# Attention's 1/sum moved to the output of a head pair, and rows normalised before their split

## The chip, the cores and the metric

The kernel runs on one core of a Trainium2 chip. The time is that of one execution in device microseconds. Five engines work side by side, each through its own queue in order: TensorE (PE: matmuls and transposes), VectorE (DVE), ScalarE (ACT), GpSimd (POOL) and SyncE (SP, which issues nearly all the DMAs here). They wait for each other by semaphores.

## The reference, cut to what matters

One encoder layer over two sequences of 512 tokens (`x_prompt` and `x_sample`, numbered 0 and 1 here) with 1024 channels: a SwiGLU feed-forward layer (FFN1), token mixing, a second feed-forward layer (FFN2), a final RMSNorm. All in fp32. What the change touches:

```python
def rms_norm(x, g):
    y = xf * lax.rsqrt(jnp.mean(xf * xf, axis=-1, keepdims=True) + EPS)
    return y * g
...
h = rms_norm(x, mix_norm)                  # x: (512, 1024) after FFN1
proj = h @ w_in                            # q, k, v, mLSTM's q, k, v, gates, o, g_att, g_mlstm
...
s = jnp.einsum('bqkgd,bskd->bkgqs', qi, k) * scale       # 8 heads of 64, 2 key/value heads
p = jax.nn.softmax(s, axis=-1)
o = jnp.einsum('bkgqs,bskd->bqkgd', p, v)
...
mem = mlstm_bidirectional(mq, mk, mv, gate_pre, mlstm_gate_bias, o_pre, mlstm_head_norm)
merged = sigmoid(g_att) * (att @ w_up_att) + sigmoid(g_mlstm) * (mem @ w_up_mlstm)
x = x + merged @ w_out
```

Both 1/rms (one number per token) and softmax's 1/sum (one per query and head) are factors that may stand before or after a matrix product.

## The kernel before

Activations lie with channels on the partitions: a tile of 128 channels by 512 tokens is a *row* here, 8 rows make a sequence. Every fp32 operand of a matmul is split into a high part in TensorE's rounded fp32 format (a copy on ACT) and the rest (a subtraction on DVE), and a product is three matmuls: high x high, high x low, low x high. `split` does this.

**FFN1's end.** `ffn_down` runs 28 steps of seven products each; `flush_` adds a bank of PSUM to the rows `xs[s]`. In the last steps the rows of sequence 0 are finished first, then those of sequence 1; `done1` is called for each finished row. It stores the row (`xbuf`, SP's queue) and adds its square to `accs[s]` (ACT squares, POOL adds, `sq_add`). For sequence 0 it also calls `emit_hl`: high part = row x gain `gm` on ACT (L144), low part by one scalar_tensor_tensor on DVE (L145), into `xh` and `xl`. So the rows are split without 1/rms. When the last row of sequence 0 is done, `mid_stats` makes 1/rms: transposes of `accs` and a sum (`col_sums`, L203 and L205), `rsqrt_cols` (Newton steps on 128x4, L171 to L192), and `bcast_cols`, which spreads it over a 128x512 row `R[s]` by four transposes (L213) and a copy (L219). `r[s]` has it by token on the partitions.

**Mixing.** `mix(s, ...)` is a generator; the two sequences are interleaved by hand (`next(m0)`, `next(m1)`), sequence 1's first projections with the end of sequence 0. The input projection runs in units: `tok_proj` puts tokens on the partitions (k/v and gates, q, mLSTM's v; lines 739 ff.), `win_cols` puts channels there (mLSTM's q and k, output gate, the two merge gates; L755). Its outputs lack 1/rms, and each eviction multiplies: with the column `r[s]` as ACT's scale in the first case, in the second by a tensor_tensor with `R[s]` on DVE (L918, L927, L1045, L1091) ahead of a split or a tanh. The weights of a unit are loaded on SP's queue, split (L239 on ACT, L240 on DVE) and parked in DRAM for sequence 1 (`load_w`).

**Attention.** `scores(h)`: for each of four blocks of 128 queries two matmuls into a PS bank, DVE's maximum (L1004), ACT's exponential with its sum (L1006), DVE's reciprocal (L1007) and DVE's scaling of the 128x512 exponentials (L1008). `attend(h)` turns them with TensorE transposes into a PT bank (L1020; there are two PT banks, also used by every other transpose), splits them, and multiplies with V into the bank `po` (L1028). The two halves of `po` are added into half of `af`, one row for a pair of heads (L1036, L1037); after the odd head `af` is split into `att`. Scores are one head ahead of `attend`. `fill` puts projection units from a queue (`att_gate`, `out_gate`) between heads.

**Order.** A list scheduler fixes each engine's order at build time, by priority; `shifted(n)` moves a part n places back. `T2(F32, "f2")` draws from a ring of four rows, `small` from rings of small tiles. In the merge of sequence 0 (`merge_mem`) `prep1` loads the rows of sequence 1 and splits them by `emit_hl`.

Of the kernel before, what the change touches and what calls it, by code (L numbers as in the profile page):

```python
# [16 lines left out]
P = 128  # L17
# [9 lines left out]
def encoder(ctx, tc, I, outs):  # L27
# [637 lines left out]
    def small(w, tag):  # L665
        return spool.tile([P, w], F32, tag=tag, bufs=2 if tag != "asm" else 6, name=nm(tag))
# [91 lines left out]
    OUT = 3  # L758

    def mix(s, xh, xl, early=None, extra=None, after=None):  # L760
# [8 lines left out]
        def F2(dtype=F32):  # L769
            return T2(dtype, "f2")  # L770

# [41 lines left out]
        def kv_done(pk):  # L813
            for b in range(4):
                nc.scalar.activation(kraw3[:, b, :], pk[b][:, 0:P], AF.Copy, scale=r[s][:, b:b + 1])
                nc.scalar.activation(Gt[:, b * 16:(b + 1) * 16], pk[b][:, 2 * P:2 * P + 16], AF.Copy,
                                     scale=r[s][:, b:b + 1])
                pv = pk[b][:, P:2 * P].rearrange("p (k e) -> p k e", k=HK)
                nc.scalar.activation(Vst[:, b, :, 0:DA], pv, AF.Copy, scale=r[s][:, b:b + 1])
                V_.scalar_tensor_tensor(Vst[:, b, :, DA:2 * DA], pv, r[s][:, b:b + 1], f(Vst[:, b, :, 0:DA]),  # L820
                                        op0=ALU.mult, op1=ALU.subtract)
# [11 lines left out]
        def q_done(pq):  # L833
            ssq = small(32, "ssq")
            for b in range(4):
                t = T2()
                nc.scalar.activation(t, pq[b], AF.Copy, scale=r[s][:, b:b + 1])
                sumsq(t, ssq[:, b * 8:(b + 1) * 8])
                qraw.append(t)
            rq.append(rstd_cols(ssq, 32, DA))  # L840
# [56 lines left out]
        def mem_values():  # L897
            def done(pvv):
                vm = A([P, 2, 4, S], F32R, "Vm")
                for b in range(4):  # L900
                    nc.scalar.activation(vm[:, 0, b, :], pvv[b], AF.Copy, scale=r[s][:, b:b + 1])
                    V_.scalar_tensor_tensor(vm[:, 1, b, :], pvv[b], r[s][:, b:b + 1], f(vm[:, 0, b, :]),
                                            op0=ALU.mult, op1=ALU.subtract)
                Vm.append(vm)
# [4 lines left out]
        def mem_qk(h, j):  # L909
            def done(pp):  # L910
# [6 lines left out]
                t = F2()  # L917
                V_.tensor_tensor(t, pp, R[s], op=ALU.mult)  # L918
                split(t, *qks[h][2 * j:2 * j + 2])
# [4 lines left out]
        def out_gate(h):  # L924
            def done(pp):
                og = T2(F32, "ac")
                V_.tensor_tensor(og, pp, R[s], op=ALU.mult)  # L927
                nc.scalar.activation(og, og, AF.Tanh, scale=0.5)
# [65 lines left out]

        def scores(h):
            hk = h // 4
            Ps = []
            for b in range(4):
# [4 lines left out]
                c = small(3, "asm")  # L1003
                V_.tensor_reduce(c[:, 0:1], p, axis=AX.X, op=ALU.max, negate=True)  # L1004
                e = T2()
                nc.scalar.activation(e, p, AF.Exp, bias=c[:, 0:1], accum_out=c[:, 1:2])  # L1006
                V_.reciprocal(c[:, 2:3], c[:, 1:2])  # L1007
                V_.tensor_scalar(e, e, c[:, 2:3], None, op0=ALU.mult)  # L1008
# [3 lines left out]
        def attend(h, Ps):  # L1012
# [25 lines left out]
            if h % 2:  # L1038
                split(af, att[:, h // 2, 0, :], att[:, h // 2, 1, :])
# [3 lines left out]
        def att_gate(d):  # L1043
            def done(pp):
                V_.tensor_tensor(mg[:, d, :], pp, R[s], op=ALU.mult)  # L1045
                nc.scalar.activation(mg[:, d, :], mg[:, d, :], AF.Tanh, scale=0.5)
# [41 lines left out]
        def mem_gate(d):  # L1088
            def done(pp):
                t = ths[d] = T2()  # L1090
                V_.tensor_tensor(t, pp, R[s], op=ALU.mult)  # L1091
                nc.scalar.activation(t, t, AF.Tanh, scale=0.5)
# [223 lines left out]
    def done1(s, d, _):  # L1316
        if s == 0:
            if d == 0:
                nhl[0] = xhl_tiles()
            emit_hl(xs[0][:, d, :], gm, d, *nhl[0])  # L1320
        nc.sync.dma_start(xbuf[s][:, d, :], xs[s][:, d, :])
        accs[s] = sq_add(xs[s][:, d, :], accs[s], "R")
        if s == 0 and d == KD - 1:
            mid_stats(0, 100, 140)
# [10 lines left out]
    def prep1(d):  # L1335
# [4 lines left out]
        emit_hl(xt, gm, d, *nhl[1])  # L1340
# [181 lines left out]
```

## Time and profile before

| what | value |
|---|---|
| median of 3 runs | 2084.76 us (2084.72 to 2087.68) |
| profiled execution, whole | 2083.45 us |
| its span in the profile | 2081.4 us |
| instructions | 27314 |
| PE busy | 2060.3 us (99%) |
| DVE busy | 1573.6 us (76%) |
| ACT busy | 895.4 us (43%) |
| POOL busy | 111.2 us (5%) |
| granted TensorE clock, mean | 0.999 |

The profile is of one execution; its times count from the start of the span. FFN1 takes the first 657 us, mixing the stretch from there to about 1431 us, FFN2 the rest. In a timeline row stand the start, the time until the end of the last of the merged instructions, engine, line and operation, the shape of output and input and the count; in brackets idle time before it and what ended it. PE's own ends are modelled, so for PE the distance from one start to the next is what a matmul costs. In a group row, after the count: busy us and mean ns of one, then the idle time of the engine ahead of it.

### The profile page before, as it was taken

To read this page: it belongs to the slowest core of one execution; us is meant where nothing else is said; L and a number is where in the kernel's file an instruction comes from. 1 tells how busy PE (TensorE), PEld (TensorE's weight loads), DVE (VectorE), ACT (ScalarE), POOL (GpSimd) and SP (SyncE) were. 2 spreads that over 40 slices of the span, in tenths; PEclk is the share of its full clock that TensorE was granted. 3 is DMA by queue.
4 is the path that set the end of the run, shared out by engine and by line. 5 is a ranking of instruction groups with operands and counts; after the bars stand their busy time and mean duration, and the time that the engine had idled before them with its cause. 6 is when DMAs were issued, how large, how long until landed. Compare 5 with 4: busy or idle time off the path is not lost.

```text
span 2081.4 us, 27314 instructions
## 1 busy us (share of the span) xinstructions
PE 2060.3 (99%) x9488; PEld 1694.0 (81%) x9488; DVE 1573.6 (76%) x2870; ACT 895.4 (43%) x1645; POOL 111.2 (5%) x122
## 2 busy tenths in 40 slices
PE   8999999999999999999999999999999999999998
PEld 6888888888888877888887788888888888888887
DVE  7888888786797899575568846555788888785797
ACT  6544444443234566463344543324444444442222
POOL 1000000001003012100120000002000000000010
PEclk9999999999999999999999999999999999999999
DMA  8656555699766655777685345677656555599753
GB/s 277 208 171 195 193 171 182 201 346 359 260 223 243 216 167 198 257 240 272 214 283 193 112 153 188 208 258 244 200 177 201 193 172 182 187 339 350 273 189 117
DMA packets 303161, 458.52 MB, mean 220 GB/s; under 512 B 20304, under 2 KB 170848, under 8 KB 302000
## 3 DMA queue, kind: packets, MB, share of 16 engines
q1 hardware_dynamic: 301152, 451.32, 64.4%
q0 software_dynamic: 1872, 5.46, 0.8%
q8 instruction: 75, 1.23, 0.2%
q14 instruction: 62, 0.51, 0.1%
HBM read 289.82 MB, written 166.89 MB: 219 GB/s over the span
## 4 chain that ended last, share of the span: by engine, by line
PE 92%; DVE 3%; DMA 3%; ACT 1%; issue 1%; SPq 0%; POOL 0%; DVEq 0%; ACTq 0%; POOLq 0%
PE mm L755 19%; PE pss L333 17%; PE pst L333 11%; PE mm L333 10%; PE mm L589 9%; PE pst L589 4%; PE pss L589 4%; PE mm L739 4%; PE pso L589 3%; PE pso L739 1%; PE pso L1028 1%; PE pso L1167 1%; PE pst L755 1%; PE pss L755 1%; PE pss L1117 1%; PE pst L1020 1%
## 5 line engine op out<-in xcount | busy, mean ns | idle before, releaser
L755 PE MATMUL mm<-xh,w 128*128 128x512 f32 x896 | 290.6, 394 | 0.0
L333 PE MATMUL pss<-xc,w 128*128 128x512 f32 x1056 | 256.4, 392 | 0.2 <-DVE t L364 0.2
L333 PE MATMUL mm<-xc,w 128*128 128x512 f32 x1056 | 253.5, 391 | 2.2 <-ACT w L291 1.4
L333 PE MATMUL pst<-xc,w 128*128 128x512 f32 x1056 | 253.8, 390 | 0.1
L333 PEld LDWEIGHTS pss<-xc,w 128*128 128x128 f32 x1056 | 197.0, 188 | 47.4 <-DVE t L364 6.7
L333 PEld LDWEIGHTS mm<-xc,w 128*128 128x128 f32 x1056 | 197.4, 188 | 45.2 <-ACT w L291 2.3
L333 PEld LDWEIGHTS pst<-xc,w 128*128 128x128 f32 x1056 | 198.2, 188 | 41.6 <-ACT t L368 0.5
L755 PEld LDWEIGHTS mm<-xh,w 128*128 128x128 f32 x896 | 167.4, 188 | 33.6
L589 PE MATMUL mm<-rt,w 128*128 128x512 f32 (+1 forms) x819 | 188.4, 385 | 0.0
L755 PE MATMUL mm<-xl,w 128*128 128x512 f32 x448 | 176.0, 393 | 0.0
L589 PEld LDWEIGHTS mm<-rt,w 128*128 128x128 f32 x819 | 151.4, 188 | 29.8
L291 ACT ACTIVATE w<-t 128x512 fp32r<-128x512 f32 x176 | 106.9, 627 | 138.6 <-issue 55.2
L292 DVE TENSOR_TENSOR w<-t,w 128x512 fp32r<-128x512 f32 x176 | 118.3, 689 | 55.1 <-ACT w L291 53.1
L333 PE MATMUL pss<-xc,f 128*128 128x512 f32 x528 | 126.9, 389 | 0.0
L333 PEld LDWEIGHTS pss<-xc,f 128*128 128x128 f32 x528 | 99.1, 188 | 20.6
L657 ACT ACTIVATE w<-wr 128x512 fp32r<-128x512 f32 x72 | 45.1, 632 | 138.6 <-PE pso L589 70.8
L657 ACT ACTIVATE w<-t 128x512 fp32r<-128x512 f32 x82 | 51.8, 632 | 107.6 <-PE pst L589 62.4
L755 PEld LDWEIGHTS mm<-xl,w 128*128 128x128 f32 x448 | 84.3, 188 | 16.7
L589 PE MATMUL pst<-rt,w 128*128 128x512 f32 x396 | 93.7, 389 | 0.0
L589 PE MATMUL pss<-rt,w 128*128 128x512 f32 x396 | 93.7, 389 | 0.0
L589 PEld LDWEIGHTS pst<-rt,w 128*128 128x128 f32 x396 | 74.3, 188 | 15.4
L589 PEld LDWEIGHTS pss<-rt,w 128*128 128x128 f32 x396 | 74.3, 188 | 15.4
(337 smaller groups left out, 3666.9 us busy)
## 6 DMA issues: line engine op xcount, KB each, us to landing
rt<-rbuf SPq DMA_DIRECT2D x154, 512.0 KB, 5.5
wpark<-w SPq DMA_DIRECT2D x104, 512.0 KB, 3.6
w<-wpark SPq DMA_DIRECT2D x104, 512.0 KB, 4.8
wr<-in_ffn_w_gate_dram SPq DMA_DIRECT2D x62, 512.0 KB, 5.3
rbuf<-tab SPq DMA_DIRECT2D x102, 256.0 KB, 3.8
wr<-in_ffn_w_up_dram SPq DMA_DIRECT2D x44, 512.0 KB, 4.7
rbuf<-f SPq DMA_DIRECT2D x72, 256.0 KB, 3.7
wr<-in_w_in_dram SPq DMA_DIRECT2D x36, 512.0 KB, 5.7
```

The source lines that it names most:

```text
L291: pin(nc.scalar.activation(t[:, 0], src, AF.Copy))
L292: pin(V_.tensor_tensor(t[:, 1], src, f(t[:, 0]), op=ALU.subtract))
L333: nc.tensor.matmul(p, a[:, k, :], xt[:, b, k, :], start=(first and k == 0 and i == 0), stop=(k == HK_ - 1 and i == 2), skip_group_check=True)
L589: nc.tensor.matmul(p, u[:, a, d * P:(d + 1) * P], r[:, b, ts], start=(first and q == 0 and k == 0), stop=(q == len(us) - 1 and k == 2), sk ...
L657: nc.scalar.activation(hi, src, AF.Copy)
L739: nc.tensor.matmul(p[b][:, :N], a[:, k, bs], w_[:, kl, :], start=(k == 0 and i == 0), stop=(k == KD - 1 and i == 2))
L755: nc.tensor.matmul(p, a[:, k, :], b, start=(k == 0 and i == 0), stop=(k == n - 1 and i == 2))
L1020: nc.tensor.transpose(p[:, b * P:(b + 1) * P], Ps[b][:, kb * P:(kb + 1) * P], ident)
L1028: nc.tensor.matmul(po, Vst[:, kv_, hk, :], w, start=(kv_ == 0 and i == 0), stop=(kv_ == 3 and i == 1))
L1117: nc.tensor.matmul(p, qk[a][:, isl], qk[b], start=(n == 0), stop=(n == 2))
L1167: nc.tensor.matmul(po, vm[:, a, t, hs_], b, start=(t == 0 and n == 0), stop=(t == 3 and n == 2))
```

## The change

- Softmax: the exponentials stay unscaled. The sums of a pair of heads go to one tile `asums` (128 x 4 blocks x 2 heads). After the odd head DVE takes one reciprocal of 128x8, ACT spreads it to a row `wide` (each value 64 times), TensorE turns that by four transposes into a PT bank, and DVE multiplies `af` with it before the split.
- `NORMED = (0, 1)`: both sequences' rows are multiplied with gain and 1/rms (`normed`, one scalar_tensor_tensor on DVE), and then split. For sequence 0 this is done for all eight rows after `mid_stats`, in place in `xs[0]`; `mid_stats` loses its shifts. For sequence 1 it is done in `prep1`.
- Evictions of the input projection lose the factor: `split_cols` is a plain split, tanh reads PSUM, mLSTM's q and k are split from PSUM.
- The ring of "asm" tiles has four buffers, was six.

```diff
@@ -663,7 +663,7 @@
     NEG = -1e30
 
     def small(w, tag):
-        return spool.tile([P, w], F32, tag=tag, bufs=2 if tag != "asm" else 6, name=nm(tag))
+        return spool.tile([P, w], F32, tag=tag, bufs=2 if tag != "asm" else 4, name=nm(tag))
 
     gm, g2 = [cpool.tile([P, KD], F32, name=nm("gain")) for _ in range(2)]
     gbias = cpool.tile([P, 16], F32, name="gbias")
@@ -756,6 +756,7 @@
         return p
 
     OUT = 3
+    NORMED = (0, 1)
 
     def mix(s, xh, xl, early=None, extra=None, after=None):
 
@@ -768,6 +769,22 @@
 
         def F2(dtype=F32):
             return T2(dtype, "f2")
+
+        def col_scale(b):
+            return 1.0 if s in NORMED else r[s][:, b:b + 1]
+
+        def split_cols(src, b, hi, lo):
+            if s in NORMED:
+                return split(src, hi, lo)
+            nc.scalar.activation(hi, src, AF.Copy, scale=r[s][:, b:b + 1])
+            V_.scalar_tensor_tensor(lo, src, r[s][:, b:b + 1], f(hi), op0=ALU.mult, op1=ALU.subtract)
+
+        def scaled_row(pp, to):
+            if s in NORMED:
+                return pp
+            t = to()
+            V_.tensor_tensor(t, pp, R[s], op=ALU.mult)
+            return t
 
         def win_cols(c0, done):
             return proj(win_v[:, :, c0:c0 + P], ("in", c0), xsrc, KD, done)
@@ -812,13 +829,11 @@
 
         def kv_done(pk):
             for b in range(4):
-                nc.scalar.activation(kraw3[:, b, :], pk[b][:, 0:P], AF.Copy, scale=r[s][:, b:b + 1])
-                nc.scalar.activation(Gt[:, b * 16:(b + 1) * 16], pk[b][:, 2 * P:2 * P + 16], AF.Copy,
-                                     scale=r[s][:, b:b + 1])
+                rsc = col_scale(b)
+                nc.scalar.activation(kraw3[:, b, :], pk[b][:, 0:P], AF.Copy, scale=rsc)
+                nc.scalar.activation(Gt[:, b * 16:(b + 1) * 16], pk[b][:, 2 * P:2 * P + 16], AF.Copy, scale=rsc)
                 pv = pk[b][:, P:2 * P].rearrange("p (k e) -> p k e", k=HK)
-                nc.scalar.activation(Vst[:, b, :, 0:DA], pv, AF.Copy, scale=r[s][:, b:b + 1])
-                V_.scalar_tensor_tensor(Vst[:, b, :, DA:2 * DA], pv, r[s][:, b:b + 1], f(Vst[:, b, :, 0:DA]),
-                                        op0=ALU.mult, op1=ALU.subtract)
+                split_cols(pv, b, Vst[:, b, :, 0:DA], Vst[:, b, :, DA:2 * DA])
             ssk = small(8, "ssk")
             sumsq(kraw, ssk)
             ko = rope_apply(kraw, rstd_cols(ssk, 8, DA), tabs[1], None)
@@ -834,7 +849,7 @@
             ssq = small(32, "ssq")
             for b in range(4):
                 t = T2()
-                nc.scalar.activation(t, pq[b], AF.Copy, scale=r[s][:, b:b + 1])
+                nc.scalar.activation(t, pq[b], AF.Copy, scale=col_scale(b))
                 sumsq(t, ssq[:, b * 8:(b + 1) * 8])
                 qraw.append(t)
             rq.append(rstd_cols(ssq, 32, DA))
@@ -898,9 +913,7 @@
             def done(pvv):
                 vm = A([P, 2, 4, S], F32R, "Vm")
                 for b in range(4):
-                    nc.scalar.activation(vm[:, 0, b, :], pvv[b], AF.Copy, scale=r[s][:, b:b + 1])
-                    V_.scalar_tensor_tensor(vm[:, 1, b, :], pvv[b], r[s][:, b:b + 1], f(vm[:, 0, b, :]),
-                                            op0=ALU.mult, op1=ALU.subtract)
+                    split_cols(pvv[b], b, vm[:, 0, b, :], vm[:, 1, b, :])
                 Vm.append(vm)
             return tok_proj(xh, xl, [(1792, 512)], 2, done)
 
@@ -914,9 +927,7 @@
                 elif s:
                     t = wpool.tile([P, 2, S], F32R, tag="wr", bufs=4, name=nm("qk"))
                     qks.setdefault(h, []).extend(t[:, i] for i in range(2))
-                t = F2()
-                V_.tensor_tensor(t, pp, R[s], op=ALU.mult)
-                split(t, *qks[h][2 * j:2 * j + 2])
+                split(scaled_row(pp, F2), *qks[h][2 * j:2 * j + 2])
             return win_cols((768, 1280)[j] + h * P, done)
 
         ogs = {}
@@ -924,8 +935,7 @@
         def out_gate(h):
             def done(pp):
                 og = T2(F32, "ac")
-                V_.tensor_tensor(og, pp, R[s], op=ALU.mult)
-                nc.scalar.activation(og, og, AF.Tanh, scale=0.5)
+                nc.scalar.activation(og, scaled_row(pp, lambda: og), AF.Tanh, scale=0.5)
                 G_.tensor_scalar(og, og, 1.0, hn[:, h:h + 1], op0=ALU.add, op1=ALU.mult)
                 ogs[h] = og
             return win_cols(2320 + h * P, done)
@@ -992,20 +1002,22 @@
         att = A([P, 4, 2, S], F32R, "att")
         afs = {}
 
+        asums = {}
+
         def scores(h):
             hk = h // 4
             Ps = []
+            if h % 2 == 0:
+                asums[h // 2] = small(8, "asum").rearrange("p (b u) -> p b u", u=2)
             for b in range(4):
                 p = PS()
                 for j in range(2):
                     nc.tensor.matmul(p, qT[:, h, b * P:(b + 1) * P], kv[:, hk * 2 + j, :],
                                      start=(j == 0), stop=(j == 1))
-                c = small(3, "asm")
-                V_.tensor_reduce(c[:, 0:1], p, axis=AX.X, op=ALU.max, negate=True)
+                c = small(1, "asm")
+                V_.tensor_reduce(c, p, axis=AX.X, op=ALU.max, negate=True)
                 e = T2()
-                nc.scalar.activation(e, p, AF.Exp, bias=c[:, 0:1], accum_out=c[:, 1:2])
-                V_.reciprocal(c[:, 2:3], c[:, 1:2])
-                V_.tensor_scalar(e, e, c[:, 2:3], None, op0=ALU.mult)
+                nc.scalar.activation(e, p, AF.Exp, bias=c, accum_out=asums[h // 2][:, b, h % 2:h % 2 + 1])
                 Ps.append(e)
             return Ps
 
@@ -1036,14 +1048,23 @@
             nc.scalar.activation(t[o0:o0 + DA, :], po[o1:o1 + DA, :], AF.Copy)
             V_.tensor_tensor(af[o0:o0 + DA, :], po[o0:o0 + DA, :], t[o0:o0 + DA, :], op=ALU.add)
             if h % 2:
-                split(af, att[:, h // 2, 0, :], att[:, h // 2, 1, :])
+                inv = asums[h // 2]
+                V_.reciprocal(inv, inv)
+                with shifted(30):
+                    wide = T2(F32, "f2")
+                    nc.scalar.activation(wide.rearrange("p (b u e) -> p b u e", u=2, e=DA),
+                                         inv.unsqueeze(3).to_broadcast([P, 4, 2, DA]), AF.Copy)
+                    pr = PT()
+                    for b in range(4):
+                        nc.tensor.transpose(pr[:, b * P:(b + 1) * P], wide[:, b * P:(b + 1) * P], ident)
+                    V_.tensor_tensor(af, af, pr, op=ALU.mult)
+                    split(af, att[:, h // 2, 0, :], att[:, h // 2, 1, :])
 
         mg = A([P, KD, S], F32, "mg")
 
         def att_gate(d):
             def done(pp):
-                V_.tensor_tensor(mg[:, d, :], pp, R[s], op=ALU.mult)
-                nc.scalar.activation(mg[:, d, :], mg[:, d, :], AF.Tanh, scale=0.5)
+                nc.scalar.activation(mg[:, d, :], scaled_row(pp, lambda: mg[:, d, :]), AF.Tanh, scale=0.5)
             return win_cols(2832 + d * P, done)
 
         queue.extend(att_gate(d) for d in range(KD))
@@ -1088,8 +1109,7 @@
         def mem_gate(d):
             def done(pp):
                 t = ths[d] = T2()
-                V_.tensor_tensor(t, pp, R[s], op=ALU.mult)
-                nc.scalar.activation(t, t, AF.Tanh, scale=0.5)
+                nc.scalar.activation(t, scaled_row(pp, lambda: t), AF.Tanh, scale=0.5)
             return win_cols(3856 + d * P, done)
 
         def merge_mem(d):
@@ -1314,14 +1334,14 @@
     box()
 
     def done1(s, d, _):
-        if s == 0:
-            if d == 0:
-                nhl[0] = xhl_tiles()
-            emit_hl(xs[0][:, d, :], gm, d, *nhl[0])
         nc.sync.dma_start(xbuf[s][:, d, :], xs[s][:, d, :])
         accs[s] = sq_add(xs[s][:, d, :], accs[s], "R")
         if s == 0 and d == KD - 1:
-            mid_stats(0, 100, 140)
+            mid_stats(0)
+            nhl[0] = xhl_tiles()
+            for k in range(KD):
+                normed(xs[0][:, k, :], gm, R[0], k)
+                split(xs[0][:, k, :], nhl[0][0][:, k, :], nhl[0][1][:, k, :])
 
     def mid_stats(s, a=0, b=0):
         with shifted(a):
@@ -1337,7 +1357,8 @@
             nhl[1] = xhl_tiles()
         xt = T2(F32, "f2")
         nc.sync.dma_start(xt, xbuf[1][:, d, :])
-        emit_hl(xt, gm, d, *nhl[1])
+        normed(xt, gm, R[1], d)
+        split(xt, nhl[1][0][:, d, :], nhl[1][1][:, d, :])
 
     ffn_down(I["ffn1_w_down"][0], rbuf[0], up.ring, tail, xbuf, done1, 7, mix_consts)
 
```

## The prediction

> **What bounds the kernel now.** I read the page first: engine shares, then the chain that ended last.
>
> ```profile
> span 2081.4 us, 27314 instructions
> PE 2060.3 (99%) x9488; PEld 1694.0 (81%) x9488; DVE 1573.6 (76%) x2870; ACT 895.4 (43%) x1645; POOL 111.2 (5%) x122
> PE 92%; DVE 3%; DMA 3%; ACT 1%; issue 1%; SPq 0%; POOL 0%; DVEq 0%; ACTq 0%; POOLq 0%
> ```
>
> TensorE (PE) is busy for 99% of the span and holds 92% of the chain. So a microsecond taken off VectorE (DVE) is worth something only where PE waits for DVE, and a microsecond added to PE, or a wait in front of it, is paid in full. The change works between the end of FFN1's down projection and the end of the token mixing; in the built order of the changed kernel PE's instructions before 642 us and those of FFN2 stand as before. Next I read the stretches of attention, of sequence 0 and of sequence 1, and the merge, in the view by windows (engine busy time, count in brackets, then clock, DMA share, GB/s).
>
> ```profile
> 700.00:820.00 120.00, 117.83 (x586) 93.69 (x585) 114.63 (x235) 72.47 (x147) 15.85 (x10) 1.00 0.57 185
> 1100.00:1200.00 100.00, 99.34 (x490) 79.81 (x489) 86.35 (x198) 51.27 (x114) 0.00 (x0) 1.00 0.42 137
> 980.00:1006.00 26.00, 26.00 (x131) 22.23 (x130) 21.72 (x28) 11.77 (x18) 9.47 (x6) 1.00 0.50 168
> ```
>
> DVE is nearly full in sequence 0's attention (114.63 of 120 us), yet PE idles only 2.17 us there and 0.66 us in sequence 1's; in the merge it never idles.
>
> **Part 1: what leaves DVE.** The groups by line:
>
> ```profile
> L1007 DVE RECIPROCAL asm<-asm 128x1 f32<-128x1 f32 x64 | 9.7, 156 | 1.4 <-ACT t L1006 1.1
> L1008 DVE TENSOR_SCALAR t<-t,asm 128x512 f32<-128x512 f32 x64 | 33.2, 522 | 0.4
> L1091 DVE TENSOR_TENSOR t<-mm,R 128x512 f32<-128x512 f32 x16 | 11.1, 691 | 46.6 <-PE mm L755 46.5
> L918 DVE TENSOR_TENSOR f<-mm,R 128x512 f32<-128x512 f32 x16 | 11.0, 687 | 21.9 <-PE mm L755 21.9
> L1045 DVE TENSOR_TENSOR mg<-mm,R 128x512 f32<-128x512 f32 x16 | 10.9, 684 | 1.0 <-PE mm L755 0.9
> L927 DVE TENSOR_TENSOR box<-mm,R 128x512 f32<-128x512 f32 x8 | 5.5, 690 | 5.5 <-PE mm L755 5.4
> L653 DVE SCALAR_TENSOR_TENSOR f<-f,gain,R 128x512 f32<-128x512 f32 x8 | 5.8, 741 | 0.0
> L1176 DVE TENSOR_TENSOR box<-box,pst 128x512 f32<-128x512 f32 x8 | 5.5, 683 | 2.9 <-PE pst L213 2.9
> L145 DVE SCALAR_TENSOR_TENSOR xl<-f,gain,xh 128x512 fp32r<-128x512 f32 x8 | 7.0, 884 | 0.0
> ```
>
> Removed: 64 reciprocals and 64 scalings of the exponentials (9.7 + 33.2 us) and the 56 products with R at lines 1091, 918, 1045 and 927 (38.5 us): 81.4 us. Added: 16 rows times 1/rms at the L653 price (11.9 us), and for each of 8 pairs a product at the L1176 price and a reciprocal (6.7 us). The low half of a row's split becomes a plain subtraction, at about the old L145 price. Net some 63 us less DVE work. How much of it does PE get? Its own waits in the mixing:
>
> ```profile
> PE pst L1020 <- DVE t L658: 1.1, 1, 1.1
> PE pso L1028 <- ACT t L657: 0.7, 2, 0.5
> PE pss L1001 <- ACT t L1006: 0.7, 1, 0.7
> ```
>
> These 2.5 us hang on DVE, directly or through the exponential (L1006) and the turned copies (L657). The ends: nothing, if other work on DVE is late in the same places; and about 16 us, if every gap between matmul starts there closed (of the attention's 220 us, PE's starts at their common pitch, 0.227 us a matmul and 0.09 a transpose, leave out that much; most of it is the switching between kinds of matmul, which stays). I take **-4 us**, near the waits, since the rows name no more.
>
> The gates' tanh and the splits of mLSTM's q and k now read PSUM directly. The bank is held until ScalarE (ACT) and, for q and k, DVE have read it, about 1.3 us in place of 0.7; a projection of 24 matmuls takes 5.4 us and three banks go round, so this is hidden. Beside that, ACT has eight copies more, at 0.6 us, over two stretches in which it idles 40%: nothing.
>
> **Part 2: what PE gets.** Each pair of heads adds four transposes of `wide`, 32 in all. What four transposes cost between matmuls is the distance of starts below: 957.93 to 958.29, 0.36 us.
>
> ```profile
> 957.71 0.39 PE L755 MATMUL mm<-xh,w 128*128 128x512 f32 x1
> 957.93 0.60 PE L213 MATMUL pst<-ident,rs 128*128 128x128 f32 x4
> 958.29 0.48 PE L755 MATMUL mm<-xh,w 128*128 128x512 f32 x1
> ```
>
> 8 x 0.36 = 2.9 us; nothing hides it on a full PE: **+3 us** (2.5 to 4). `wide` also takes one of the two PT banks from the transposes' start to DVE's product (about 1.5 us per pair) beside the turning of the next head's exponentials. The queue of gate projections covers that; without cover it is up to 8 x 1.5 = 12 us (rival C).
>
> **Part 3: the start of mixing, sequence 0.** Before, rows are split unscaled as they leave the down projection, and 1/rms is needed only when the first projection is evicted. Now sums, 1/rms, R, eight products and eight splits stand between the last row and the first matmul. What is there now, on PE, then on the others:
>
> ```profile
> 639.99 6.28 PE L589 MATMUL mm<-rt,w 128*128 128x512 f32 x27
> 654.76 2.20 PE L589 MATMUL pso<-rt,w 128*128 128x512 f32 x9
> 656.80 0.41 PE L739 MATMUL mm<-w,xh 128*128 128x272 f32 x2
> 669.35 0.29 PE L739 MATMUL pso<-w,xl 128*128 128x272 f32 x1
> 669.78 0.50 PE L739 MATMUL mm<-w,xh 128*128 128x512 f32 x1
> ```
>
> ```profile
> 642.16 0.68 DVE L606 SCALAR_TENSOR_TENSOR xs<-pst,xs 128x512 f32<-128x512 f32 x1
> 643.50 0.62 ACT L155 ACTIVATE f<-xs 128x512 f32<-128x512 f32 x1
> 641.88 1.52 POOL L156 TENSOR_TENSOR R<-R,f 128x512 f32<-128x512 f32 x1 [0.85 <-ACT f L155]
> 653.17 0.68 DVE L205 TENSOR_REDUCE cs<-pst 128x4 f32<-128x512 f32 x1
> 653.89 0.17 DVE L162 TENSOR_SCALAR rs<-cs 128x4 f32<-128x4 f32 x1
> 656.55 0.16 DVE L192 SCALAR_TENSOR_TENSOR rs<-rs,rs 128x4 f32<-128x4 f32 x1
> 657.65 0.68 DVE L606 SCALAR_TENSOR_TENSOR xs<-pso,xs 128x512 f32<-128x512 f32 x1
> 658.25 0.71 DVE L240 TENSOR_TENSOR w<-wr,w 128x544 fp32r<-128x544 f32 x1
> 659.78 0.69 DVE L219 COPY R<-pst 128x512 f32<-128x512 f32 x1 [0.81 <-PE pst L213]
> wr<-in_w_in_dram SPq DMA_DIRECT2D x36, 512.0 KB, 5.7
> ```
>
> (The L240 row at 658.25 is one weight of half width; DVE's starts follow at 0.60 us, 0.66 where the instruction takes a gain too.) The built order of the changed kernel puts the column sums' transposes (L203) on PE behind the first 9 matmuls of the step that begins at 639.99, and those of 1/rms (L213) 17 matmuls later. Worked through:
> - PE reaches L203 at 642.0. The last row of sequence 0 is flushed by 640.9 (the split that held it until 642.16 is gone), squared by 641.6, added on GpSimd (POOL, 1.52) by 643.1: PE waits **1.1 us**.
> - L203 0.36, 17 matmuls 3.85: PE is at L213 at 647.4. DVE, from 643.7: the reduction 0.7, twelve small steps in some 2.2 (653.89 to 656.7, less a flush), a flush 0.6: 647.3. No long wait. L213 ends at 648.0.
> - DVE: R 0.7, a flush 0.6, then eight products (5.3), eight subtractions (4.9) and a half weight (0.7), all ahead of the flush of bank `pso` of that same step: 660.3, flushed at 660.9.
> - PE: the rest of that step (10 matmuls) until 650.3, three banks of the last step (27 matmuls, 6.1) until 656.4; the fourth accumulates in `pso` and has to wait for its flush: **4.5 us**. Behind it wait the mixing's first matmuls. Nine matmuls: 662.9, against 656.8 before.
> - The last flushes, queued on DVE behind this, hold the fourth bank of the k/v projection until about 665. That projection takes 12.5 us before with four transposes inside, some 12 now: end at 675.2 (669.5 before).
> - SyncE's queue is in order. The second weight of the q projection is now issued behind stores that wait for DVE's late weight splits: about 670, landing 5.7 later, split at 678.5. The new PE order wants it after six matmuls: about **1 us**.
>
> Sum: q begins 6.1 us later and waits 1 us: **+7.2 us**. Nothing later gives it back on a full PE. Ends: 4, if DVE's sixteen steps overlap more closely; 11, if the weights come a full landing (5.7) late in place of 1.
>
> Sequence 1's rows are scaled in the merge of sequence 0 (the window 980 to 1006). R for it exists since head 2, four row buffers let four of the eight products go ahead of the window, and DVE has 26 - 21.7 = 4.3 us left in it for the other four (3.0): hidden, and four PSUM banks go round in front of DVE. Without that cover it is at most all eight, 5.9 us. The fewer "asm" buffers cost nothing: a bank's exponential comes before its next maximum anyway.
>
> **Sum.** -4 + 3 + 7.2 = +6.2 us. The profiled run took 2083.45 us (2.05 around its span), so 2089.65 by it, a span of 2087.6. The median of the runs shown is 2084.76, 1.3 above the profiled run, so the same sum gives **2091.0**.
>
> **Rivals.**
> - *A, the relief is larger.* Place: the attention, where PE's starts lose 16 us in all. If half of the loss hangs on DVE's queue and not on switching, -10 in place of -4: 2085.0, no difference. It decides from -6.1 on (2088.9); with all 16 and the boundary at its low end (4 + 3 - 16) it is 2075.8, faster. For: DVE at 96% in 700 to 820. Against: only 2.83 us of idle PE there.
> - *B, the clock falls in the hole.* PE's idle stretch of 4.5 us is longer than any in the middle of the trace. The rows of the trace's two ends:
>
> ```profile
> 12.35 1.06 PE L1238 MATMUL pss<-ident,raw 128*128 128x128 f32 x4
> 14.45 0.60 PE L1238 MATMUL mm<-ident,raw 128*128 128x128 f32 x4
> 2070.00:2075.00 5.00, 2.42 (x18) 1.78 (x17) 4.93 (x28) 2.18 (x9) 0.00 (x0) 1.00 0.36 134
> 2075.00:2081.00 6.00, 0.00 (x0) 0.00 (x0) 2.16 (x9) 1.33 (x2) 0.00 (x0) 0.55 0.63 238
> ```
>
>   At the end the granted clock is at its half some 3 us after PE's last work (2.42 us busy, then 0.55 over six); at the start four transposes take 1.06 us until about 14, then 0.60. So the hole can halve the clock, and the work until it is back, taken as 4 us, loses 2: 2093.0. [...]
> - *C, the pair's product stalls the turning.* PT is taken and PE waits each time: +12 in place of nothing, 2103.0. Against: the built order puts gate matmuls around each set.
> - *D, the hole is not there*: DVE is so far ahead that it ends the flush before 656.4. It needs 4.5 us less of 17 us of DVE work in a row whose durations the rows show: 2086.5, no difference.
>
> **Chances.** Forecast 0.42, B 0.22, A 0.20 (0.12 faster, 0.08 the same), D 0.10, C 0.06. About 0.2% (4.2 us) is what a measurement here can tell from no change: below 2080.6 is faster, above 2088.9 slower. Slower 0.70, the same 0.18, faster 0.12. The range, 2084 to 2099, leaves out A's faster part, C, and little else; it takes in the boundary's ends (2087.8 and 2094.8) and B on top of them.
>
> **What would show it.** PE's first L739 matmul near 663 and q's near 677; a PE wait for DVE at the last step's `pso`; the 16 products with R between 649 and 661; in 700 to 820 less DVE (near 90 us) but hardly fewer us per matmul. Wrong: no hole at 656 (then D), the mixing behind it, 680 to 1431 in the trace of before, shorter by over 3 us (A), clock under 1.00 at 660 (B), or PE idle before the new transposes (C).

## The result, and the profile after

The changed kernel took **2107.09 us** (median of 4, 2105.87 to 2108.40) against 2084.85 before: a ratio of 1.0104, 95% interval [1.0091, 1.0116], 22 us slower. The forecast was 2091.0. The profiled execution took 2106.74 us, its span 2104.8. The page's lines after, answering to those of before:

```profile
span 2104.8 us, 27262 instructions
PE 2071.1 (98%) x9520; PEld 1697.0 (81%) x9520; DVE 1530.0 (73%) x2718; ACT 892.2 (42%) x1653; POOL 106.7 (5%) x122
PE 86%; DVE 4%; issue 4%; DMA 4%; ACT 1%; POOL 0%; SPq 0%; DVEq 0%; ACTq 0%; POOLq 0%
```

DVE is 43.6 us less busy, PE has its 32 transposes more, and the share of PE in the chain fell from 92 to 86%. Of the 23.4 us that the span grew, 12.6 are PE standing still (33.7 us of the span in place of 21.1) and 10.8 are PE being busy for longer, with the transposes and with matmuls at half the clock. To find where, I took four landmarks that both orders share, PE's first matmul of the q projection and of mLSTM's V projection in each sequence (line 739, 512 columns). The distances between them in the profiled executions; all later tables use the same four:

| kernel | q(0) starts | q(0) to V(0), attention of 0 | V(0) to q(1), merge of 0 | q(1) to V(1), attention of 1 | median us |
|---|---|---|---|---|---|
| before | 669.78 | 159.16 | 185.28 | 200.80 | 2084.85 |
| after | 679.28 | 164.62 | 184.82 | 209.44 | 2107.09 |
| difference | +9.5 | +5.5 | -0.5 | +8.6 | +22.2 |

Outside these stretches the two traces differ by under 0.6 us. In the first one stands the forecast hole (timeline of after, PE, then DVE):

```profile
643.65 0.66 PE L203 MATMUL pst<-ident,R 128*128 128x128 f32 x4 [0.89 <-POOL R L156]
...
650.83 6.28 PE L589 MATMUL mm<-rt,w 128*128 128x512 f32 x27
662.46 4.08 PE L589 MATMUL pso<-rt,w 128*128 128x512 f32 x9 [5.35 <-DVE xs L606]
666.38 0.41 PE L739 MATMUL mm<-w,xh 128*128 128x272 f32 x2
...
648.72 0.69 DVE L219 COPY R<-pst 128x512 f32<-128x512 f32 x1 [0.74 <-PE pst L213]
...
649.92 3.12 DVE L653 SCALAR_TENSOR_TENSOR xs<-xs,gain,R 128x512 f32<-128x512 f32 x3
...
660.52 1.28 DVE L658 TENSOR_TENSOR xl<-xs,xh 128x512 fp32r<-128x512 f32 x2
661.73 0.68 DVE L606 SCALAR_TENSOR_TENSOR xs<-pso,xs 128x512 f32<-128x512 f32 x1
```

PE waits 5.35 us for a flush that DVE has queued behind sixteen products and subtractions. Nine matmuls at `pso` then take 3.92 us (662.46 to 666.38) in place of 2.04: the clock was halved, as the windows show (last columns: clock, DMA share, GB/s).

```profile
655.00:660.00 5.00, 2.11 (x10) 1.42 (x8) 5.00 (x9) 2.53 (x4) 0.00 (x0) 0.94 0.00 0
660.00:665.00 5.00, 2.54 (x6) 2.06 (x7) 4.84 (x8) 2.52 (x5) 1.65 (x2) 0.50 0.68 219
```

What was not forecast stands in the attention of both sequences. PE's waits there (700 to 862, then 1060 to 1242; total, times, longest):

```profile
PE pst L213 <- DVE rs L192: 2.1, 1, 2.1
PE pst L1032 <- DVE f L1060: 1.0, 1, 1.0
PE pso L1040 <- DVE t L658: 0.3, 1, 0.3
PE pst L1059 <- ACT f L1055: 0.2, 1, 0.2
...
PE pss L1015 <- ACT t L1020: 3.0, 1, 3.0
...
```

These waits are only a part. Of the 5.5 and 8.6 us, four sets of transposes in each sequence are 1.4 (4 x 0.36, the price in the prediction's rows); PE's idle time grew by 1.8 us in sequence 0 (160.62 us busy of 164.62, before 156.97 of 159.16) and by 3.3 in sequence 1; and behind the 3.0 us wait 3.4 us of PE's work ran at half the clock, a loss of 1.7. In each sequence some 2.2 us are left that no wait names.

The 3.0 us are at sequence 1's first scores. What DVE did ahead of it:

```profile
1126.68 0.50 PE L1015 MATMUL pss<-kv,qT 128*128 128x512 f32 x1 [3.00 <-ACT t L1020]
...
1123.86 0.69 DVE L977 TENSOR_TENSOR box<-box,tab 128x512 f32<-128x512 f32 x1 [1.56 <-DMA box<-ebuf]
1124.47 0.68 DVE L658 TENSOR_TENSOR qk<-mm,qk 128x512 fp32r<-128x512 f32 x1
1125.07 1.28 DVE L1018 TENSOR_REDUCE asm<-pss 128x1 f32<-128x512 f32 x2
```

The scores' first maxima (L1018) stand in DVE's queue behind an addition over a row of mLSTM (L977) whose row is still on its way from memory. The built order of the changed kernel has four such additions ahead of the first maximum (at 1114.01, 1118.36, 1120.42 and 1123.86); that of before had two (L967 at 1101.48 and 1103.88). Both banks of scores are taken, so PE waits for the exponential, which waits for the maximum, which waits for a row that has nothing to do with it.

### The profile page after: what moved, and what is told of

It reads as the page before. It is cut to its first block, busy times and chain, and to the rows that moved or that the text cites. A ratio compares the mean times of both kernels' runs of the same rounds, so it can differ in the third digit from the quotient of the medians.

```text
span 2104.8 us, 27262 instructions
## 1 busy us (share of the span) xinstructions
PE 2071.1 (98%) x9520; PEld 1697.0 (81%) x9520; DVE 1530.0 (73%) x2718; ACT 892.2 (42%) x1653; POOL 106.7 (5%) x122
## 4 chain that ended last, share of the span: by engine, by line
PE 86%; DVE 4%; issue 4%; DMA 4%; ACT 1%; POOL 0%; SPq 0%; DVEq 0%; ACTq 0%; POOLq 0%
PE pss L333 17%; PE mm L755 17%; PE pst L333 11%; PE mm L589 8%; PE mm L333 8%; PE pst L589 4%; PE pss L589 4%; PE mm L739 3%; PE pso L589 3%; PE pso L1040 1%; PE pso L1187 1%; DMA wr<-in_ffn_w_gate_dram 1%; PE pso L739 1%; PE pss L1137 1%; PE pst L755 1%
## 5 line engine op out<-in xcount | busy, mean ns | idle before, releaser
L755 PE MATMUL mm<-xh,w 128*128 128x512 f32 x896 | 294.1, 395 | 0.0
L755 PEld LDWEIGHTS mm<-xh,w 128*128 128x128 f32 x896 | 167.6, 188 | 33.3
L755 PE MATMUL mm<-xl,w 128*128 128x512 f32 x448 | 176.2, 393 | 0.0
L240 DVE TENSOR_TENSOR w<-wr,w 128x1024 fp32r<-128x1024 f32 (+1 forms) x56 | 71.2, 1272 | 48.7 <-ACT w L239 48.5
L755 PEld LDWEIGHTS mm<-xl,w 128*128 128x128 f32 x448 | 84.5, 189 | 16.9
L658 DVE TENSOR_TENSOR t<-pst,t 128x512 fp32r<-128x512 f32 x96 | 64.3, 686 | 34.5 <-ACT t L657 26.1
```

Of the source, the lines that this page charges most:

```text
L240: pin(lo_eng.tensor_tensor(lo, raw, f(hi), op=ALU.subtract))
L658: (eng or V_).tensor_tensor(lo, src, f(hi), op=ALU.subtract)
L755: nc.tensor.matmul(p, a[:, k, :], b, start=(k == 0 and i == 0), stop=(k == n - 1 and i == 2))
```

## The experiments

Theory, after the result: **queue order**. DVE's lighter load is worth nothing to PE; the new order of instructions makes a few places in which PE waits behind something that DVE's queue holds, and most of these come with the normalisation half. Rival: **pair product**, the softmax half costs the 14 us in attention by its transposes, bank and chain. Medians beside the stage lengths of the profiled execution (the start of q(0) varies by about 1 us between profiles of the same order, see after, e4 and e6). The runs were taken in several rounds, and the median of before in them was 2084.85 (with after), 2085.00 (e1 to e4), 2085.49 (e5 to e8), 2084.64 (e9 to e11) and 2084.11 (e12), so a difference between kernels of different rounds is uncertain by about 1 us:

| kernel | q(0) starts | attention 0 | merge 0 | attention 1 | median us |
|---|---|---|---|---|---|
| e1 softmax half | 670.65 | 160.36 | 185.44 | 204.24 | 2089.83 |
| e2 normalisation half | 679.55 | 162.74 | 184.90 | 209.80 | 2102.48 |
| e3 flush first | 674.58 | 164.57 | 184.81 | 211.16 | 2101.82 |
| e4 rows behind | 680.08 | 165.53 | 184.87 | 203.39 | 2107.32 |
| e5 no division | 669.49 | 161.23 | 185.43 | 201.71 | 2088.14 |
| e6 rows spread | 678.91 | 165.36 | 184.98 | 204.21 | 2100.94 |
| e7 = e3 + e6 | 673.59 | 164.75 | 184.92 | 204.28 | 2096.00 |
| e8 sequence 1 only | 669.93 | 159.82 | 184.68 | 201.54 | 2084.52 |
| e9 = e7, later 1/rms | 674.47 | 164.25 | 184.85 | 205.57 | 2096.96 |
| e10 = e7, rows of 0 on DVE | 676.34 | 160.86 | 186.28 | 204.20 | 2092.79 |
| e11 normalisation, moved | 675.38 | 163.57 | 184.90 | 201.51 | 2091.34 |
| e12 = e8, rows of 0 on DVE | 669.63 | 154.50 | 186.82 | 201.86 | 2080.70 |

**e1, the softmax half alone.**

```
-    NORMED = (0, 1)
+    NORMED = ()
```

With it `done1` and `prep1` split the unscaled rows as before.

> Only the softmax half of the change; rows and evictions as before. Theory 'queue order' (the loss sits in a few holes that the new instruction order makes, and most of these belong to the normalisation half): the start of mixing as before (first q matmul near 670), no 2 us wait of PE at the transposes of sequence 1's 1/rms (its order has 18 gate matmuls ahead of them, 11 in the changed kernel), no 3 us wait at the first scores of sequence 1 (two row additions stand ahead of the first maximum on DVE, four in the changed kernel); left are the 32 transposes (2.9 us) and about 1.5 us of small waits: 2088 to 2090. Rival 'pair product' (attention's extra 13.9 us come from the softmax half: transposes, the PT bank, the product in front of the turned copies): 2084.9 + 13.9 = about 2099.

2089.83 us, ratio 1.0021 [1.0012, 1.0031]: queue order's number; the rival's 2099 is out. Neither the 2.1 nor the 3.0 us wait is there.

**e2, the normalisation half alone** (scores and attend as before).

> Only the normalisation half; softmax as before, with 1/sum on the exponentials. Queue order: the hole at bank pso and the late start of mixing as in the changed kernel (9.8 us; first q matmul near 679), and the wait at sequence 1's first scores (its DVE order has the same four row additions ahead of the first maximum; 3.2 us of wait and 1.9 us of halved clock against 0.7 before): 2084.9 + 9.8 + 4.4 = about 2099. Pair product: only the start of mixing, 2094.7.

2102.48 us, ratio 1.0083 [1.0068, 1.0098]. The two halves add up, 4.8 + 17.5 = 22.3 us, and four fifths are the normalisation's. It is 3.5 above the number expected. In the profiled execution (which ran 4 us over the median) the wait at sequence 1's first scores is 5.1 us in place of the 3.2 counted on, and attention of sequence 0 has 3.5 us of waits for the split of turned exponentials that I had not counted:

```profile
PE pss L1011 <- ACT t L1016: 5.3, 2, 5.1
PE pst L1030 <- DVE t L658: 3.5, 3, 1.9
```

**e3, the flush ahead of the products.**

```
             for k in range(KD):
-                normed(...); split(...)
+                with shifted(150):
+                    normed(...); split(...)
```

> The whole change; sequence 0's eight products and splits are given a later due time (150), so DVE's order has the flush of bank pso of the last step but one right behind the first product. Queue order: the 5.4 us wait of PE at pso goes, and with it the halved clock, PE follows the rows as they come: first q matmul near 672 in place of 679.3, time about 2107 - 7 = 2100. Rival 'the rows are late whatever the order' (the hole moves to the first matmuls of the mixing, which need the rows): 2105 to 2108, with PE waiting for DVE at the first mixing matmuls for 4 us or more.

2101.82 us, 5.3 less than after (5.4 by before of the same rounds). The 5.35 us wait is gone, and with it the half clock at 660. The mixing's first matmuls wait 2.5 us in two places, again for flushes (L606) of FFN1's last banks that stand behind products and splits, and not for the rows themselves. So it was the order of DVE's queue.

```profile
661.95 0.52 PE L739 MATMUL mm<-w,xh 128*128 128x272 f32 x2 [1.51 <-DVE xs L606]
664.45 0.52 PE L739 MATMUL pso<-w,xh 128*128 128x272 f32 x2 [0.98 <-DVE xs L606]
```

**e4, sequence 1's rows behind head 4.**

```
+            pin = tc.keep_in_program_order if s else (lambda i: i)
-            V_.tensor_reduce(n1[:, d, :, h], em3, axis=AX.X, op=ALU.max)
+            pin(V_.tensor_reduce(n1[:, d, :, h], em3, axis=AX.X, op=ALU.max))
```

The other maximum and the addition (L977) are pinned in the same way.

> The whole change; in sequence 1 the additions and maxima over mLSTM's rows (lines 977, 982, 983) are kept in program order on DVE, behind attention's head 4, in place of ahead of the first maxima of the scores. Queue order: PE's 3.0 us wait at sequence 1's first scores and the halved clock behind it go: 2107 - 4.4 = about 2102.7, less what the rows cost where they stand then (nothing, if DVE has room: 79 of 100 us from 1140 to 1240). Rival 'the scores wait for something else' (the splits of mLSTM's q, or the clock): 2106 to 2108, with the wait at the first scores still over 2 us.

2107.32 us: no gain, the number of the rival, but not by its reason. The wait at the first scores is gone (attention of 1: 203.39 in place of 209.44), and a new one stands behind V(1): the late rows stop DVE at 1238.7, and mLSTM's first products hang on what is queued behind them. From V(1) to the end this kernel takes 5.0 us more than after.

```profile
1240.93 0.69 DVE L977 TENSOR_TENSOR box<-box,tab 128x512 f32<-128x512 f32 x1 [2.25 <-DMA box<-ebuf]
...
1245.55 1.65 PE L1138 MATMUL pss<-qk,qk 128*128 128x512 f32 x3 [2.23 <-DVE t L1154]
```

**e6, the rows head by head behind heads 0 to 3**, with e4's pins.

```
-            if h >= 4:
-                mem_max(h - 4, 0)
-                mem_max(h - 4, 1)
+            first = 0 if s else 4
+            if first <= h < first + 4:
+                mem_max(h - first, 0)
+                mem_max(h - first, 1)
```

> The whole change; sequence 1's mLSTM rows are taken head by head behind attention's heads 0 to 3, in program order on DVE, neither ahead of the first maxima nor all behind head 4. Theory 'DVE's queue stood still for a row on its way from memory, with the first maxima behind it': the wait at the first scores goes as in e4 and none comes back at the first mLSTM products: 2107.1 - 5.5 = about 2101.6. Rival 'a row that is late stops DVE wherever it stands': 2105 to 2108, with a new wait of PE of 2 us or more somewhere from 1130 to 1260.

2100.94 us, 6.1 less than after (6.8 by before of the same rounds). From 1060 to 1260 PE's whole list of waits is now

```profile
PE pst L904 <- DVE et L900: 0.4, 1, 0.4
PE pst L951 <- DVE t L658: 0.3, 2, 0.2
```

**e7, the edits of e3 and e6 together.**

> The whole change with both moves of order, e3's later products and e6's rows. If the two holes are separate costs, the gains add: 2107.1 - 5.3 - 5.5 = about 2096.3. What is left over before is then 2.9 us of transposes, some 5 us at the start of mixing and 3 us of waits in sequence 0's attention. If one hides behind the other: 2100 to 2102.

2096.00 us, 11.1 less than after (11.7 by before of the same rounds): the two holes are separate costs and add up.

**e5, e1 without the division by the sums.**

```
-                inv = asums[h // 2]
-                V_.reciprocal(inv, inv)
...
-                    V_.tensor_tensor(af, af, pr, op=ALU.mult)
```

> The softmax half alone, without the division by the sums (no reciprocals, no wide tile, no transposes, no pair product; the output isn't divided): DVE is 43 us lighter than before and PE has no instruction more. What it differs from before is what PE gets of the relief; what e1 (2089.8) is longer is the price of the pair's product. Theory 'PE hardly waits for DVE there': relief 0 to 2 us, so 2083 to 2087, and the product costs its 32 transposes (2.9 us) and little else. Rival 'the relief is worth 4 us or more' (as predicted): 2081 or less, and the product with its transposes costs 9.

2088.14 us, ratio 1.0012 [1.0002, 1.0021]. DVE does 28 us less (1545.3 in its page, by overlapping busy time), PE executes what it did before, and the kernel is 2.7 us longer (0.4 to 4.4 by the interval), not shorter. Attention of sequence 0 has 2.1 us of that. The prediction's rows of such waits came to 2.5 us; here two alone come to 3.9:

```profile
PE pss L1015 <- ACT t L1020: 2.0, 2, 1.3
PE pst L1032 <- DVE t L658: 1.9, 2, 1.3
```

So the relief is worth nothing or less, outside both theories' numbers. Why these waits grew is not taken apart: a new order on DVE would do it, and no run shows that it did; the shorter ring of "asm" tiles, which e1 and e5 keep, was not run by itself either. The pair product with its 32 transposes costs e1 - e5 = 1.7 us by the medians, 2.2 by before of the same rounds.

**e8, sequence 1 alone normalised**, softmax and `done1` as before, rows as in e6.

```
-    NORMED = (0, 1)
+    NORMED = (1,)
```

> Only sequence 1's rows are normalised before their split (sequence 0 and softmax as before), with e6's order of the rows. Theory 'hidden in the merge, and nothing to be had from DVE': 2083 to 2087, as before. Rival 'the eight products in the merge are paid' (5.9 us): about 2091. If DVE's relief in sequence 1 is worth something to PE, 2082 or less.

2084.52 us, ratio 0.9994 [0.9984, 1.0003]: no difference. The eight products in the merge are hidden (its merge takes 184.68 us, before 185.28), and there is nothing to be had; what e6's order of the rows does to it by itself was not run.

**e9, e7 with sequence 1's 1/rms one head later.**

```
-            if h == 2 and extra:
+            if h == 3 and extra:
```

> e7 with sequence 1's 1/rms and its R asked for behind head 3 of sequence 0's attention in place of head 2: the order has 38 gate matmuls (11 in e7) on PE ahead of the transposes of 1/rms, and the last steps of 1/rms stand behind no row. Theory 'PE's wait at these transposes is a cost of its own' (2.1 to 2.6 us of wait, and in e7 some 1.5 us more of halved clock): 2096.0 - 2.2 to - 4 = 2092 to 2094. Rival 'it hides another wait' (the turned exponentials behind it): 2095 to 2097.

2096.96 us, ratio 1.0060 [1.0045, 1.0075]: the rival's number. The wait only moved: 1.6 us at L213, and 1.0 at the exponentials behind it.

**e10, e7 with sequence 0's row additions on DVE.**

```
-            (G_, V_)[s].tensor_tensor(em3, ...)
+            V_.tensor_tensor(em3, ...)
```

In the changed kernel, DVE and GpSimd around the 2.1 us wait at L213:

```profile
772.46 1.29 POOL L977 TENSOR_TENSOR box<-box,tab 128x512 f32<-128x512 f32 x1 [8.40 <-DMA box<-ebuf]
774.63 2.06 POOL L977 TENSOR_TENSOR box<-box,tab 128x512 f32<-128x512 f32 x1 [0.88 <-DMA box<-ebuf]
...
772.95 0.81 DVE L189 SCALAR_TENSOR_TENSOR rs<-rs 128x4 f32<-128x4 f32 x1
775.49 1.22 DVE L192 SCALAR_TENSOR_TENSOR rs<-rs,rs 128x4 f32<-128x4 f32 x1
...
776.86 0.62 PE L213 MATMUL pst<-ident,rs 128*128 128x128 f32 x4 [2.08 <-DVE rs L192]
```

Steps over four columns take 0.81 and 1.22 us and end 0.01 and 0.02 us after the addition on GpSimd does.

> e7 with the additions over sequence 0's mLSTM rows on DVE in place of GpSimd (eight instructions, 5.5 us more on DVE). In the changed kernel and in e7 single steps of sequence 1's 1/rms of four columns take 0.8 to 1.2 us where others take 0.16, each ending with an addition on GpSimd. Theory 'an addition on GpSimd holds up a DVE step with two operands in SBUF': every such step takes under 0.2 us, and PE's wait at the transposes of 1/rms is under 1.5 us (2.6 in e7); time 2094 to 2096. Rival 'these steps wait for something on DVE itself': steps of 0.8 us and more remain.

2092.79 us, 3.2 less than e7, which ran in other rounds; by before of the same rounds it is 2.4 (ratios 1.0042 [1.0027, 1.0057] and 1.0047 [1.0032, 1.0062]), not clear of noise. What is clear is that the long steps are gone: the longest of them (min/median/max ns behind the count) is 156 ns, and the wait at L213 is gone, although DVE has sixteen instructions more (2734 in place of 2718; eight additions stand ahead of the maxima, as expected, and mLSTM's heads make eight more):

```profile
L189 DVE SCALAR_TENSOR_TENSOR rs<-rs x3: 145/149/156, 765.6 to 770.3; 128x4 f32<-128x4 f32 x3
L192 DVE SCALAR_TENSOR_TENSOR rs<-rs,rs x3: 147/153/154, 767.0 to 771.7; 128x4 f32<-128x4 f32 x3
```

Attention of sequence 0 takes 3.9 us less than in e7 and its merge 1.4 more. The profiled execution of e10 ran 2.6 us over the median; its clock was at half from 664.96 to 668.37, at the start of mixing, which costs it 1.7 us and makes its q(0) late.

**e11, the normalisation half with the moves of e3, e6 and e9.**

> The normalisation half alone (softmax as before), with all three moves of order: the later products of e3, the rows of e6 and the later 1/rms of e9. If the softmax half costs what it cost alone (e1: 4.8 us), this is e9 less 4.8: 2087 to 2089, and what is left over before is the start of mixing (some 4 us). If the softmax half's lighter DVE is what keeps the other half cheap: as e9 or longer, 2092 and more.

2091.34 us, ratio 1.0034 [1.0022, 1.0045]. Its number was built on the 2092 to 2094 expected of e9; against the measured e9 it is 5.6 less, near the 4.8 of e1. The softmax half is a cost of its own beside this one too.

**e12, e8 with e10's edit**, the candidate.

> e8 (sequence 1 alone normalised, rows head by head) with sequence 0's row additions on DVE as in e10, the two edits that cost nothing or gained: a candidate against before (2084.6 to 2085.5). If DVE's steps that GpSimd holds up reach PE's waits in sequence 0's attention (about 2 us in e8's profile), 2082 to 2083.5. If they are hidden there, or the 5.5 us more on DVE make up for them: 2084 to 2086.

2080.70 us against 2084.11 in the same rounds, ratio 0.9984 [0.9975, 0.9993]: 3.4 us under the kernel before, and more than expected. Its attention of sequence 0 takes 154.50 us (159.82 in e8, 159.16 before) and its merge 186.82 (184.68 in e8), as some of PE's work moved from the first to the second (771 instructions in place of 777 in the first); the two together are 3.2 us shorter than in e8. PE's waits from 630 to 1430 are down to

```profile
PE pss L1127 <- DVE t L1143: 0.6, 1, 0.6
PE pst L951 <- DVE t L658: 0.4, 2, 0.3
PE pst L904 <- DVE et L900: 0.4, 1, 0.4
PE pso L1039 <- ACT t L657: 0.2, 1, 0.2
```

## Why the prediction was right or wrong

The direction was right, the size far off: +6.2 us forecast, +22.2 measured, above the range.

- **Part 1, the relief (-4 us): the step that failed.** In attention the profile shows +5.5 and +8.6 where -4 and +3 were to stand, 15 us off. The work that leaves DVE was forecast well (63 us; by single durations 60.8 left, of which the page shows 43.6 since its instructions overlap). What failed is the step from there to PE: that PE's waits could only shrink, with ends of 0 to -16. A loss was left out, and no row excluded one. In its place stand new waits of PE for DVE's queue in its new order. e5 measures softmax's relief by itself as +2.7 us; e2 shows that the normalisation half alone brings the order with the 3.0 to 5.1 us wait at sequence 1's first scores and 3.6 us more in sequence 0's attention; and e6, which only moves the rows on DVE, gains 6.1 us. That it is DVE's lighter load that makes the planner choose this order is argued, not shown. I had compared the two built orders only at the boundary, where the change visibly adds steps, and had taken attention's order as given. That most of the 16 us at PE's starts is switching between kinds of matmul was my estimate and is not shown: in before, from 700 to 820 and 1100 to 1200, the start that follows a matmul at L755 comes 0.232 us after it by the median where it is of another line (111 times) and 0.227 where it is of the same (434).
- **Part 2, the transposes (+3): about right.** e1 - e5 is 1.7 us by the medians, 2.2 by before of the same rounds. By stages it is uneven: 2.5 more in sequence 1's attention (204.24 against 201.71) and 0.9 less in sequence 0's (160.36 against 161.23). Rival C's stall came at one place of eight: 1.0 us at L1032 behind L1060.
- **Part 3, the start of mixing (+7.2): the mechanism right, the size short.** The wait for GpSimd was 0.9 us (1.1 forecast), the hole 5.35 (4.5), the products and subtractions ran from 649.9 to 661.8 (649 to 661), L739 began at 666.38 (663), q at 679.28 (677). Of the 2.3 us missing at q, the half clock is 1.9 (3.92 against 2.04 us for nine matmuls), and the flush ended 1.5 later than forecast (662.4, not 660.9). Against that, the forecast 1 us for the second q weight hardly came: PE's list of waits from 600 to 700 holds two more only, 0.9 at L203 and 0.6 at `pso`. e3 confirms the mechanism by taking it away. Sequence 1's products were hidden, as forecast (merge -0.5; e8).
- **Rivals.** B happened, and at its price of 2 us: the clock was at 0.50 from 660 to 665. The 4 us that B takes until the clock is back were my estimate, and nothing in before shows them; in after they are 3.8 (662.46 to 666.26). But its 2093.0 is still 14 us short, and the clock fell a second time in attention, at 1127.06, where no rival had put it. A is refuted for the softmax half by e5, D by the hole. That PE's losses in attention can be had back shows only in e12, in part as work moved to the merge, and there by moving work onto DVE. A rival was missing: that a lighter engine is given its work in another order.
- **Signals.** DVE in 700 to 820 is at 95.9 us (near 90 forecast). There was no PE idle of size ahead of the new transposes (0.2 us). The stretch from q(0) to V(1) grew by 13.6 us, where A had asked for 3 less.

What stays open: which of the planner's choices in sequence 0's attention costs what. After e3, e6 and e10 the whole change is still 8 us over before; the start of mixing holds some 4 of them where the clock holds (q(0) is 3.8 us late in e7, 4.7 in e9) and 6.6 in e10's own profile, where it fell, and the softmax half's 4.8 (e1) overlap with the rest in a way not taken apart.

## What to carry to other kernels

When the order of instructions comes from a planner, taking work off an engine that isn't the bound also moves everything else in its queue: compare the orders over the whole region, and look for each in-order queue in which something that waits for memory now stands ahead of something the bound needs. Give the relief of such an engine a loss as one of its ends. And look at what a helper engine does to its neighbour: sixteen additions moved from GpSimd onto the busier DVE gained about 2.4 us in two kernels (in e10 not clear of noise), where 28 us less work on DVE gained nothing.

## What the runs showed of the hardware

**Steps on DVE took longer beside an addition on GpSimd.** In the rows at 772 to 777 above, steps whose two operands lie in SBUF end with GpSimd's addition. e7 has a reduction with one operand beside such an addition, at its usual 0.69 us, and behind it a step with two, which again ends with GpSimd's (767.55 and 767.53):

```profile
766.24 1.29 POOL L977 TENSOR_TENSOR box<-box,tab 128x512 f32<-128x512 f32 x1 [8.82 <-DMA box<-ebuf]
...
766.13 0.69 DVE L984 TENSOR_REDUCE st<-box 128x4 f32<-128x512 f32 x1 [1.14 <-DMA box<-ebuf]
766.73 0.82 DVE L189 SCALAR_TENSOR_TENSOR rs<-rs 128x4 f32<-128x4 f32 x1
```

Of the three steps at L192 in after, one took 1.22 us, beside GpSimd's addition, and the median is 0.16. It is not only steps with two operands: where softmax still scales its exponentials on DVE (one 128x512 operand in SBUF and a column), four of the 64 scalings took 0.86 to 1.45 us in e8, each beside an addition on GpSimd, in place of 0.48 (in before four too, 847 to 1465 ns); in e12, with these additions on DVE, the longest of the 64 took 0.49. What it costs the kernel is shown roughly: e10 is 2.4 us under e7 and e12 2.4 under e8, by before of the same rounds, and moving the additions changed the order of both too.

**The clock fell after much shorter holes than rival B's 4.5 us.** The holes of PE over 1.8 us in the middle of the profiled executions, by length: 5.35 or 5.36 (after, e2, e4, e6), 5.14 (e2), 5.09 (e3), 3.00 (after), 2.56 (e7), 2.23 and 2.16 (e4) and 1.90 (e3) came with a stretch at half the clock; 2.13 (e6), 2.08 (after), 1.87 (e2) and 1.83 (e11) did not. In e10 and e11 the clock also fell behind two short waits in a row at the start of mixing, 1.49 and 0.98 us, which e7 and e9 have too without a fall. Before, e1, e5, e8 and e12 have no hole over 1.8 us and no fall.

So six of the thirteen falls came behind a hole of over 5 us and seven without one, and a hole of 2.13 us passed where one of 1.90 did not: the length alone does not tell. The traces also show what goes with a fall. In the middle of the executions the stretches at half the clock are 3.41 or 6.83 us long, and within one execution they start a whole number of 3.41 us apart (659.43 and 1127.06 in after are 137 of them). So one can lay windows of 3.41 us on that grid and count how long PE stood idle in each. First e3, whose hole of 1.90 us lies in one window, then after, whose hole of 2.08 us at the same wait lies across two:

```profile
768.91:772.33 3.42, 1.52 (x11) 1.12 (x10) 3.42 (x5) 0.02 (x1) 1.97 (x1) 1.00 0.72 280
772.33:775.74 3.41, 3.41 (x11) 2.61 (x10) 2.71 (x5) 1.18 (x2) 1.28 (x1) 0.50 0.84 261
...
775.48:778.89 3.41, 2.03 (x14) 1.83 (x15) 3.41 (x6) 0.60 (x1) 2.12 (x2) 1.00 0.99 337
778.89:782.30 3.41, 3.41 (x22) 2.82 (x21) 3.41 (x7) 1.68 (x3) 0.39 (x1) 1.00 0.74 225
```

PE (the first busy time) idles 1.90 us of the first window, and the next is at half the clock; it idles 1.38 us of the third, and the next is not. So it is in all fourteen traces: the window ahead of each of the thirteen falls has PE idle for 1.66 us (e10, 661.54 to 664.96) to all of it, and no window with 1.60 us idle (e9, 781.00 to 784.41) or less was followed by a fall. In between stands one window with 1.75 us (e2, 760.74 to 764.16) without one. In these runs, then, every fall followed a window in which PE was idle for about half of the 3.41 us or more, and where a hole lay on the grid counted beside its length: 1.90 us in one window (e3) with a fall, 2.08 us across two (after) without.
